# Three edits to a fp32-split streaming encoder step: queue order in the SSD chunks, block order at the start of the FFN, and the end of the last norm

## The chip, the cores and the metric

The kernel runs on one NeuronCore of one Trainium2 chip. The metric is the device time of one execution in microseconds (us). Five engines work side by side, each through its own instruction queue in order: PE (matmul; its weight loads are listed apart as PEld), DVE (VectorE), ACT (ScalarE), POOL (GpSimd) and SP (SyncE, which here only issues DMAs).

## The reference

One layer of a hybrid encoder for a prompt of 1040 rows (16 meta rows and 1024 frames) and for 8 running streams of 16 frames each, 1168 rows in all, width 1024. Stick-breaking attention and a Mamba-2 SSD branch read the same normed input, are merged with gates, and a convolutional FFN and a last norm follow. What the edits touch:

```python
# SSD branch, per chunk and head (decay exponents are <= 0)
decay_ts = exp(where(causal, a_cum[t] - a_cum[s], -inf))
y_diag   = einsum(C·B masked * decay_ts * dt[s], x)
chunk_states = einsum(to_end, B, x)            # the state's product
h        = chunk_decay * h + chunk_states      # carried from chunk to chunk
y        = y_diag + C·h_in·exp(a_cum) + d_skip * x
# FFN and last norm
u  = rms_norm(h, g_ffn);  up = causal_dwconv(u @ w_up)     # gate and val, 2816 columns each
h  = h + (silu(gate) * val) @ w_down
y  = rms_norm(h, g_final)
```

## The kernel before, in words

All large products are made of three matmuls in a rounded format: every operand is split into a high and a low part, and high·high, high·low and low·high are accumulated (`mm3`, L115, L118 and L119). A weight block of 128 columns is loaded by SP (L104), its high part made by ACT (L105) and its low part by DVE (L106). One product of such a block with a third of the rows is 24 matmuls.

The code is written for a tile framework. It plans the order of every engine's queue ahead of time: it runs the program through a simulated timeline with its own costs, and lets each engine take the instruction that is ready, earlier lines of the program first. The queues are fixed then. At run time an engine that reaches an instruction whose input has not come waits there, and all that is queued behind waits with it. Buffers of a pool are handed on in the same way: `bufs=1` or `bufs=2` says how many tiles of a name can live at a time. `issue_after(ins, prev)` adds an edge without a semaphore: the planner may not place `ins` before `prev`. Before the change it is used between instructions of one engine only.

The phases in order of time: the input norm and projections (to about 100 us), four SSD groups (to about 875 us), attention for the prompt (to about 1480 us), attention for the running streams, the merge, the output projection, the FFN (from about 2152 us) and the last norm with the output.

An SSD group convolves six blocks of 128 channels (B, C and four of x), then walks through ten chunks: the running streams' rows (chunk 9) first, then chunks 0 to 8 of the prompt, and between them `sample_state`. The large products of `z_proj` (gates) and of the next group's convolution blocks are what PE can do in between; they are called fill here. `ssd_chunk` does, in program order, with the names that the trace shows:

- L448: DMA of the exponents' rows into tile `t` (in the code `R`; four buffers, shared with `sample_state`)
- L450: C·B and the transpose of B into the PSUM tile `ms`; L454 (DVE): the masked product `cb`; L456 (ACT): the copy `bt` of B
- the transposes of x into `px` (one buffer); L462 (DVE) `xd`, L464 (POOL) `xe`
- L473 (PE): `st`, the state's product, of `xe` and `bt`; L479 (POOL) and L481 (DVE): the new state `hs`
- L483 (ACT): eight Relu instructions that clip the exponents, one per head; L484 (ACT): their Exp; L485 (DVE): the product with `cb`
- L488 (PE): `yd`; L493 and L494: DMA of `e`; L497 (PE) `yo`; L498 to L501 (DVE): the sum into x.

`out_proj(i)` makes a third of the rows of the residual, sums their squares (L1077 on ACT, L1078 on POOL), gets the inverse root (L1084, L1086, L1087) and splits the normed input of the FFN (`ph`, `pl`). `ffn_up(j)` makes block j of the gate (e = 0) and of the value (e = 1) for the three thirds. Its products go through four PSUM buffers `mm`. `ffn_last` is the last group of down projections: for each third i, eight blocks m are added to the residual (L1176), squared and summed (L1074, L1077, L1078), multiplied by the gain (L1198), transposed (`tp`, L135) and copied (L1206). Then the sum over channels is made by PE (`ss`, L1212), the inverse root by ACT and DVE (L1215 to L1217 and the four small DVE instructions of `refine`, L174 to L177), the result is scaled in three column pieces q by DVE, ACT and POOL (L1224, L1227) and written by SP (L1230, L1232).

Of the kernel before, what the change touches and what calls it, by code (L numbers as in the profile page):

```python
# [13 lines left out]
F32 = mybir.dt.float32  # L14
F32R = mybir.dt.float32r
# [62 lines left out]
class Kernel:  # L78
# [362 lines left out]
    def ssd_chunk(self, g, ch, t0, n, BT, CT, X, Hs):  # L441
# [11 lines left out]
        msk = (self.blockc if smp else self.causal)[:n, :n]  # L453
        nc.vector.tensor_tensor(out=CB[:, 0, :], in0=pc[:n, :n], in1=msk, op=ALU.mult)  # L454
        Bt = self.tile(sb, [128, 128], F32, 'bt')[:n]
        nc.scalar.copy(Bt, pc[:n, 128:256])  # L456
        px = self.tile(ps, [128, 512], F32, 'px')
        for j in range(4):
            self.T_(px[:n, 128 * j:128 * j + 128], X[j][:, ts])
# [6 lines left out]
        if smp:  # L466
            Bm = self.tile(sb, [128, 8, 128], F32, 'bm', bufs=1)
            nc.gpsimd.tensor_tensor(out=Bm, in0=Bt.unsqueeze(1).to_broadcast([128, 8, 128]),
                                    in1=self.blk.unsqueeze(2).to_broadcast([128, 8, 128]), op=ALU.mult)
        else:  # L470

            pS = self.tile(ps, [128, 512], F32, 'st')
            nc.tensor.matmul(pS, Bt, xe.rearrange("p h d -> p (h d)"), start=True, stop=True)  # L473
            Hn = self.tile(sb, [128, 512], F32, 'hs', bufs=2)
            if ch == 0:
                nc.vector.tensor_copy(Hn, pS)
            else:
                hv = lambda t: t.rearrange("p (h d) -> p h d", d=64)
                nc.gpsimd.tensor_tensor(out=hv(Hn), in0=hv(Hs), op=ALU.mult,  # L479
                                        in1=self.dec[:, ch, h0:h0 + 8].unsqueeze(2).to_broadcast([128, 8, 64]))  # L480
                nc.vector.tensor_tensor(out=Hn, in0=pS, in1=Hn, op=ALU.add)  # L481
        for h in range(8):
            nc.scalar.activation(R[:, h, :], R[:, h, :], AF.Relu, scale=-1.0, bias=tk[:, h0 + h:h0 + h + 1])  # L483
        nc.scalar.activation(R, R, AF.Exp, scale=-1.0)  # L484
        nc.vector.tensor_tensor(out=R, in0=R, in1=CB.to_broadcast([n, 8, n]), op=ALU.mult)  # L485
        yd = self.tile(ps, [128, 4, 128], F32, 'yd')
# [626 lines left out]
    def ffn_up(self, j, u2):  # L1113

        nc, a, fp = self.nc, self.a, self.fp
        cs = self.tile(fp, [128, 2, 18], F32, 'cs')
        fs = self.tile(fp, [16, 2, 128], F32, 'fs', bufs=1)
        nc.sync.dma_start(fs, a['state_ffn_conv'][0].rearrange("b i c -> (b i) c")
                          .rearrange("r (e c) -> r e c", e=2)[:, :, 128 * j:128 * j + 128])
        pf = self.tile(self.pf, [128, 512], F32, 'tp')  # L1120
        for e in range(2):
            self.T_(pf[:, 16 * e:16 * e + 16], fs[:, e])
        fi = self.tile(fp, [128, 32], F32, 'fi')
        nc.scalar.copy(fi, pf[:, :32])
        ac, act = [], []
        for e in range(2):
            blk = j + 22 * e
            w = lambda q: self.cwf[:, q * 44 + blk:q * 44 + blk + 1]
            ac.append(self.tile(fp, [128, 3, 384], F32, 'acc', bufs=3))
            W = self.weights(a['w_up'][0], 0, 8, DFF * e + 128 * j, 128)  # L1130
            for i in range(3):
                n0 = PW if i < 2 else 258
                x = self.tile(fp, [128, 402], F32, 'fx', bufs=3)
                xs = x[:, n0:].rearrange("p (b t) -> p b t", t=18) if i == 2 else None

                def evac(p, c, w_):
                    nc.scalar.copy(x[:, :n0], p[:, :n0])
                    if i == 2:
                        nc.scalar.copy(xs[:, :, 2:18], p[:, n0:w_].rearrange("p (b t) -> p b t", t=16))
                self.proj(W, u2[i], [(0, PW)], evac)  # L1140
                o = ac[e][:, i]
                parts = [(o[:, 0:n0 - 2], lambda q: x[:, q:q + n0 - 2])]
                if i == 2:
                    nc.gpsimd.tensor_copy(xs[:, :, 0:2], fi[:, 16 * e:16 * e + 16].rearrange("p (b i) -> p b i", i=2))
                    nc.gpsimd.tensor_copy(cs[:, e, 0:2], x[:, n0 - 2:n0])
                    nc.gpsimd.tensor_copy(cs[:, e, 2:18].rearrange("p (b i) -> p b i", i=2), xs[:, :, 16:18])
                    parts.append((o[:, 256:384].rearrange("p (b t) -> p b t", t=16), lambda q: xs[:, :, q:q + 16]))
                for op, src in parts:
                    nc.scalar.activation(op, src(0), AF.Identity, scale=w(0), bias=w(3))  # L1149
                    for q in (1, 2):  # L1150
                        nc.vector.scalar_tensor_tensor(out=op, in0=src(q), scalar=w(q), in1=op, op0=ALU.mult, op1=ALU.add)  # L1151
                if e == 0:
                    nc.scalar.activation(o, o, AF.Silu)
                    continue
                nc.vector.tensor_tensor(out=ac[0][:, i], in0=ac[0][:, i], in1=o, op=ALU.mult)
                act.append(tuple(self.tile(self.actp, [128, 384], F32R, n) for n in ('ah', 'al')))
                self.split(*act[i], ac[0][:, i])
        p = self.tile(self.pf, [128, 512], F32, 'tp')
        for e in range(2):
            self.T_(p[:18, 128 * e:128 * e + 128], cs[:, e, :])  # L1160
        so = self.tile(fp, [18, 256], F32, 'so', bufs=1)
        nc.scalar.copy(so, p[:18, :256])
        for e in range(2):
            cc = slice(DFF * e + 128 * j, DFF * e + 128 * j + 128)
            nc.sync.dma_start(a['ffn_conv_prompt'][0, 0][:, cc], so[0:2, 128 * e:128 * e + 128])
            nc.sync.dma_start(a['ffn_conv_sample'][0].rearrange("b i c -> (b i) c")[:, cc], so[2:18, 128 * e:128 * e + 128])
        return act
# [18 lines left out]
    def ffn_last(self, j0, act):  # L1186

        nc, a, fp = self.nc, self.a, self.fp
        for i in range(3):
            c = 384 * i  # L1190
            ss, ys, last, n = self.tile(self.pf, [128, 512], F32, 'ss', bufs=1), [], None, 0
            acc = self.tile(fp, [128, PW], F32, 'sq')[:, :384]
            for m in range(8):
                if m % 2 == 0:
                    W = self.weights(a['w_down'][0], j0, len(act), 128 * m, 256)
                h = self.down(W, act, m, i)
                self.square(acc, h, m == 0)
                nc.vector.tensor_scalar(out=h, in0=h, scalar1=self.gv[:, 24 + m:25 + m], scalar2=None, op0=ALU.mult)  # L1198
                prev, last = last, h
                for h in ([] if m == 0 else [prev]) + ([last] if m == 7 else []):  # L1200
                    pt = self.tile(self.pf, [128, 512], F32, 'tp')
                    for b in range(3):
                        self.T_(pt[:, 128 * b:128 * b + 128], h[:, 128 * b:128 * b + 128])
                    if n % 3 == 0:
                        ys.append(self.tile(fp, [128, 3, 384], F32, 'acc', bufs=3))
                    done = nc.scalar.copy(ys[-1][:, :, 128 * (n % 3):128 * (n % 3) + 128],  # L1206
                                          pt[:, :384].rearrange("p (b n) -> p b n", n=128))
                    if n == 3:
                        self.load_sqrt(fp, done)
                    n += 1  # L1210
            for b in range(3):
                nc.tensor.matmul(ss[:, b:b + 1], acc[:, 128 * b:128 * b + 128], self.ones[:, 0:1], start=True, stop=True)  # L1212
            t = self.tile(fp, [128, 2, 3], F32, 'nrm')
            s, r = t[:, 0], t[:, 1]
            nc.scalar.copy(s, ss[:, 0:3])  # L1215
            nc.scalar.activation(r, s, AF.Sqrt, bias=self.eps, scale=1.0 / D)
            nc.vector.reciprocal(r, r)  # L1217
            self.refine(fp, r, s, 1.0 / D)
            for q, y in enumerate(ys):
                k = min(384, D - 384 * q)  # L1220
                y = y[:, :, :k]
                if q == 1:
                    for b in range(3):
                        nc.scalar.activation(y[:, b], y[:, b], AF.Copy, scale=r[:, b:b + 1])  # L1224
                else:
                    eng = nc.vector if q == 0 else nc.gpsimd
                    eng.tensor_tensor(out=y, in0=y, in1=r.unsqueeze(2).to_broadcast([128, 3, k]), op=ALU.mult)  # L1227
                cs = slice(384 * q, 384 * q + k)
                nb = 3 if i < 2 else 2
                nc.sync.dma_start(a['y_prompt'][0][c:c + 128 * nb, cs].rearrange("(b p) n -> p b n", p=128), y[:, :nb])  # L1230
                if i == 2:
                    nc.sync.dma_start(a['y_sample'].rearrange("b t c -> (b t) c")[:, cs], y[:, 2])  # L1232


def body(ctx, tc, a):
# [41 lines left out]
```

## Time and profile before

| what | value |
|---|---|
| median of three runs | 3040.69 us (3036.63 to 3044.58) |
| the profiled execution | 3035.7 us, its span 3033.7 us |
| mean granted TensorE clock | 0.988 |
| busy: PE, DVE, ACT, POOL | 2926.8, 1733.1, 1262.9, 611.2 us |
| HBM traffic | 244.31 MB read, 91.15 MB written |

Times in the rows are microseconds from the start of the span. In a list of waits the columns are: the engine and what it wanted to do, what ended its wait, the sum, the count and the longest. In a timeline: start, duration, engine, line, operation, output and inputs, count, and in brackets the idle time of the engine before it and what ended it. In a table of windows: busy time of each engine with the number of its instructions, then the granted clock, the busy share of the DMA engines and GB/s.

### The profile page before, as it was taken

The numbers are of one execution on the slowest core, as the hardware profiler recorded it, in microseconds if no ns is written. First come the engines' busy times: TensorE is split into PE (matmuls) and PEld (weight loads), VectorE is DVE, ScalarE is ACT, GpSimd is POOL, SyncE is SP. The second block draws the span as 40 slices with busy tenths as digits, with TensorE's granted clock in tenths as the row PEclk, the third lists the DMA queues.
The fourth block names the chain that finished last, engine by engine and source line by source line (L and its number), as shares of the span: only waits on it lengthen the run. The fifth ranks groups of instructions, "written<-read, shape, count | busy, mean of one in ns | idle before, by whom it ended". The sixth has DMA issues, their size and how long they took to land. (4 is left out here: it accounts for less than half of the span.)

```text
span 3033.7 us, 45461 instructions
## 1 busy us (share of the span) xinstructions
PE 2926.8 (96%) x17381; PEld 2768.3 (91%) x17381; DVE 1733.1 (57%) x2625; ACT 1262.9 (42%) x2630; POOL 611.2 (20%) x967
## 2 busy tenths in 40 slices
PE   7999999999989999999799899999999999999998
PEld 5997988979879999999699899999999999999997
DVE  6467666666656777777634441346754454545447
ACT  6545435354334544554434320214534242424245
POOL 0013132131222333333323000002201010101014
PEclk9999999999999999999899999999999999999999
DMA  5436255353574554544444553536211111111113
GB/s 188 110 86 172 87 141 152 91 162 90 148 218 125 167 148 132 157 124 106 77 137 140 168 171 100 152 105 195 71 43 44 43 44 43 44 43 40 39 43 119
DMA packets 445496, 338.44 MB, mean 112 GB/s; under 512 B 43991, under 2 KB 421155, under 8 KB 445279
## 3 DMA queue, kind: packets, MB, share of 16 engines
q1 hardware_dynamic: 445279, 335.54, 38.8%
q8 instruction: 137, 2.24, 0.3%
q14 instruction: 80, 0.66, 0.1%
HBM read 244.31 MB, written 91.15 MB: 111 GB/s over the span
## 5 line engine op out<-in xcount | busy, mean ns | idle before, releaser
L115 PE MATMUL mm<-sh,wh 128*128 128x384 f32 (+3 forms) x2520 | 869.5, 346 | 14.7 <-ACT sh L942 5.2
L118 PE MATMUL mm<-sl,wh 128*128 128x384 f32 (+3 forms) x2520 | 869.8, 345 | 2.3 <-DVE sl L98 1.2
L119 PE MATMUL mm<-sh,wl 128*128 128x384 f32 (+3 forms) x2520 | 865.6, 344 | 0.0
L115 PEld LDWEIGHTS mm<-sh,wh 128*128 128x128 f32 (+1 forms) x2520 | 475.7, 189 | 29.5 <-ACT sh L942 6.4
L118 PEld LDWEIGHTS mm<-sl,wh 128*128 128x128 f32 (+1 forms) x2520 | 475.7, 189 | 15.5 <-issue 8.9
L119 PEld LDWEIGHTS mm<-sh,wl 128*128 128x128 f32 (+1 forms) x2520 | 475.5, 189 | 5.7 <-issue 3.9
L106 DVE TENSOR_TENSOR wl<-wf,wh 128x1024 fp32r<-128x1024 f32 (+2 forms) x205 | 252.6, 1233 | 318.0 <-ACT wh L105 317.8
L115 PE MATMUL mm<-ph,wh 128*128 128x386 f32 x1248 | 424.5, 340 | 2.7 <-ACT ph L97 2.0
L118 PE MATMUL mm<-pl,wh 128*128 128x386 f32 x1248 | 424.6, 341 | 0.0
L119 PE MATMUL mm<-ph,wl 128*128 128x386 f32 x1248 | 422.5, 339 | 0.2 <-DVE wl L106 0.2
L105 ACT CAST wh<-wf 128x1024 fp32r<-128x1024 f32 (+2 forms) x205 | 212.4, 1037 | 482.2 <-PE mm L118 454.5
L1151 DVE SCALAR_TENSOR_TENSOR acc<-fx,cwf,acc 128x256 f32<-128x256 f32 (+1 forms) x352 | 170.8, 516 | 154.0 <-ACT acc L1149 150.0
L115 PEld LDWEIGHTS mm<-ph,wh 128*128 128x128 f32 x1248 | 236.2, 189 | 3.9 <-ACT ph L97 2.3
L119 PEld LDWEIGHTS mm<-ph,wl 128*128 128x128 f32 x1248 | 236.2, 189 | 1.1 <-DVE wl L106 0.7
L118 PEld LDWEIGHTS mm<-pl,wh 128*128 128x128 f32 x1248 | 235.2, 188 | 1.8
L686 DVE TENSOR_TENSOR_SCAN keep<-keep 128x144 f32<-128x144 f32 (+7 forms) x128 | 179.7, 1406 | 57.9 <-POOL keep L685 57.2
L115 PE MATMUL mm<-ah,wh 128*128 128x384 f32 x528 | 179.8, 340 | 0.0
L119 PE MATMUL mm<-ah,wl 128*128 128x384 f32 x528 | 179.2, 339 | 0.0
L118 PE MATMUL mm<-al,wh 128*128 128x384 f32 x528 | 178.6, 338 | 0.0
L1078 POOL TENSOR_TENSOR sq<-sq,sq 128x386 f32<-128x386 f32 (+1 forms) x42 | 60.2, 1434 | 467.9 <-ACT sq L1077 456.4
L98 DVE TENSOR_TENSOR wTl<-wT,wTh 128x512 fp32r<-128x512 f32 (+3 forms) x176 | 103.0, 602 | 80.1 <-ACT wTh L97 79.1
L1176 DVE TENSOR_TENSOR h<-mm,h 128x384 f32<-128x384 f32 x144 | 79.8, 556 | 119.7 <-PE mm L119 119.5
(329 smaller groups left out, 4548.2 us busy)
## 6 DMA issues: line engine op xcount, KB each, us to landing
wf<-in_w_in SPq DMA_DIRECT2D x80, 512.0 KB
wf<-in_w_up SPq DMA_DIRECT2D x44, 512.0 KB
t<-s_ac SPq DMA_DIRECT2D x36, 512.0 KB
wf<-in_w_down SPq DMA_DIRECT2D x28, 512.0 KB
wf<-in_w_out SPq DMA_DIRECT2D x24, 512.0 KB
s_y<-x SPq DMA_DIRECT2D x16, 577.0 KB
yt<-s_y SPq DMA_DIRECT2D x16, 577.0 KB
KH<-s_kh SPq DMA_DIRECT2D x32, 260.0 KB
```

What stands on the lines that cost most here:

```text
L98: nc.vector.tensor_tensor(out=l, in0=x, in1=h.bitcast(F32), op=ALU.subtract)
L105: nc.scalar.copy(wh, wf)
L106: nc.vector.tensor_tensor(out=wl, in0=wf, in1=wh.bitcast(F32), op=ALU.subtract)
L115: i = nc.tensor.matmul(p, wh[:, k, :], mh[:, c:c + w], start=s, stop=False)
L118: nc.tensor.matmul(p, wh[:, k, :], ml[:, c:c + w], start=False, stop=False)
L119: nc.tensor.matmul(p, wl[:, k, :], mh[:, c:c + w], start=False, stop=e)
L686: nc.vector.tensor_tensor_scan(out=K[:, ::-1], data0=K[:, ::-1], data1=K[:, ::-1], initial=1.0, op0=ALU.mult, op1=ALU.min)
L1078: nc.gpsimd.tensor_tensor(out=acc[:, :w], in0=acc[:, :w], in1=sq, op=ALU.add)
L1151: nc.vector.scalar_tensor_tensor(out=op, in0=src(q), scalar=w(q), in1=op, op0=ALU.mult, op1=ALU.add)
L1176: self.nc.vector.tensor_tensor(out=h, in0=p, in1=h, op=ALU.add)
```

## The change

In `ssd_chunk` each of the eight Relu instructions gets an ordering edge: in the nine prompt chunks behind the state's product `st` of the same chunk, which is an instruction of PE; in the running streams' chunk behind the copy `bt`.

In `ffn_up` the two `acc` tiles and the two weight blocks (gate and value) are requested together ahead of the loop, for every j. For j = 0 the six products are made in the order gate third 0, gate third 1, value third 0, value third 1, gate third 2, value third 2; for the other j the order is as before.

In `ffn_last`, block m = 7 is no longer added to the sum of squares by POOL: PE accumulates the sum of m < 7 and the square of m = 7 into `ss` with twice the matmuls. The gain of m = 7 is applied by ACT in place of DVE. The copy of `ss` to SBUF (L1215) goes; the root and the refinement read PSUM. Piece q = 2 of the result is scaled by POOL (one of three row blocks) and DVE (two) in place of POOL alone, and the writes of piece q = 1 are issued by ACT in place of SP.

```diff
-        nc.scalar.copy(Bt, pc[:n, 128:256])
+        first = nc.scalar.copy(Bt, pc[:n, 128:256])
...
-            nc.tensor.matmul(pS, Bt, xe.rearrange("p h d -> p (h d)"), start=True, stop=True)
+            first = nc.tensor.matmul(pS, Bt, xe.rearrange("p h d -> p (h d)"), start=True, stop=True)
...
         for h in range(8):
-            nc.scalar.activation(R[:, h, :], R[:, h, :], AF.Relu, scale=-1.0, bias=tk[:, h0 + h:h0 + h + 1])
+            self.issue_after(nc.scalar.activation(R[:, h, :], R[:, h, :], AF.Relu, scale=-1.0,
+                                                  bias=tk[:, h0 + h:h0 + h + 1]), first)
...
-        ac, act = [], []
-        for e in range(2):
+        act = []
+        ac = [self.tile(fp, [128, 3, 384], F32, 'acc', bufs=3) for e in range(2)]
+        W = [self.weights(a['w_up'][0], 0, 8, DFF * e + 128 * j, 128) for e in range(2)]
+
+        for e, i in ((0, 0), (0, 1), (1, 0), (1, 1), (0, 2), (1, 2)) if j == 0 else ((e, i) for e in range(2) for i in range(3)):
...
-                self.square(acc, h, m == 0)
-                nc.vector.tensor_scalar(out=h, in0=h, scalar1=self.gv[:, 24 + m:25 + m], scalar2=None, op0=ALU.mult)
+                if m < 7:
+                    self.square(acc, h, m == 0)
+                    nc.vector.tensor_scalar(out=h, in0=h, scalar1=self.gv[:, 24 + m:25 + m], scalar2=None, op0=ALU.mult)
+                else:
+
+                    sq = self.tile(fp, [128, PW], F32, 'sq')[:, :384]
+                    nc.scalar.activation(sq, h, AF.Square)
+                    for b in range(3):
+                        for x, e in ((acc, False), (sq, True)):
+                            nc.tensor.matmul(ss[:, b:b + 1], x[:, 128 * b:128 * b + 128], self.ones[:, 0:1], start=not e, stop=e)
+                    nc.scalar.activation(h, h, AF.Copy, scale=self.gv[:, 31:32])
...
-            for b in range(3):
-                nc.tensor.matmul(ss[:, b:b + 1], acc[:, 128 * b:128 * b + 128], self.ones[:, 0:1], start=True, stop=True)
-            t = self.tile(fp, [128, 2, 3], F32, 'nrm')
-            s, r = t[:, 0], t[:, 1]
-            nc.scalar.copy(s, ss[:, 0:3])
+            s, r = ss[:, 0:3], self.tile(fp, [128, 3], F32, 'nrm')
...
-                    eng = nc.vector if q == 0 else nc.gpsimd
-                    eng.tensor_tensor(out=y, in0=y, in1=r.unsqueeze(2).to_broadcast([128, 3, k]), op=ALU.mult)
+                    for eng, b, e in ((nc.vector, 0, 3),) if q == 0 else ((nc.gpsimd, 2, 3), (nc.vector, 0, 2)):
+                        eng.tensor_tensor(out=y[:, b:e], in0=y[:, b:e], op=ALU.mult,
+                                          in1=r[:, b:e].unsqueeze(2).to_broadcast([128, e - b, k]))
...
-                nc.sync.dma_start(a['y_prompt'][0][c:c + 128 * nb, cs].rearrange("(b p) n -> p b n", p=128), y[:, :nb])
+                dma = nc.scalar if q == 1 else nc.sync
+                dma.dma_start(a['y_prompt'][0][c:c + 128 * nb, cs].rearrange("(b p) n -> p b n", p=128), y[:, :nb])
                 if i == 2:
-                    nc.sync.dma_start(a['y_sample'].rearrange("b t c -> (b t) c")[:, cs], y[:, 2])
+                    dma.dma_start(a['y_sample'].rearrange("b t c -> (b t) c")[:, cs], y[:, 2])
```

More of the change, by code (lines that the diff above doesn't have):

```diff
@@ L1124, in ffn_up @@
         nc.scalar.copy(fi, pf[:, :32])
-        ac, act = [], []
-        for e in range(2):
+        act = []
+        ac = [self.tile(fp, [128, 3, 384], F32, 'acc', bufs=3) for e in range(2)]
+        W = [self.weights(a['w_up'][0], 0, 8, DFF * e + 128 * j, 128) for e in range(2)]
+        for e, i in ((0, 0), (0, 1), (1, 0), (1, 1), (0, 2), (1, 2)) if j == 0 else ((e, i) for e in range(2) for i in range(3)):
             blk = j + 22 * e
             w = lambda q: self.cwf[:, q * 44 + blk:q * 44 + blk + 1]
[L1129 to L1142, printed above, removed]
-                if i == 2:
[L1144 to L1157, printed above, removed]
@@ new lines, in ffn_up, with evac @@
+            n0 = PW if i < 2 else 258
+            x = self.tile(fp, [128, 402], F32, 'fx', bufs=3)
+            xs = x[:, n0:].rearrange("p (b t) -> p b t", t=18) if i == 2 else None
+            def evac(p, c, w_):
+                nc.scalar.copy(x[:, :n0], p[:, :n0])
+                if i == 2:
+                    nc.scalar.copy(xs[:, :, 2:18], p[:, n0:w_].rearrange("p (b t) -> p b t", t=16))
+            self.proj(W[e], u2[i], [(0, PW)], evac)
+            o = ac[e][:, i]
+            parts = [(o[:, 0:n0 - 2], lambda q: x[:, q:q + n0 - 2])]
@@ new lines, in ffn_up @@
+            if i == 2:
+                nc.gpsimd.tensor_copy(xs[:, :, 0:2], fi[:, 16 * e:16 * e + 16].rearrange("p (b i) -> p b i", i=2))
+                nc.gpsimd.tensor_copy(cs[:, e, 0:2], x[:, n0 - 2:n0])
+                nc.gpsimd.tensor_copy(cs[:, e, 2:18].rearrange("p (b i) -> p b i", i=2), xs[:, :, 16:18])
+                parts.append((o[:, 256:384].rearrange("p (b t) -> p b t", t=16), lambda q: xs[:, :, q:q + 16]))
+            for op, src in parts:
+                nc.scalar.activation(op, src(0), AF.Identity, scale=w(0), bias=w(3))
+                for q in (1, 2):
+                    nc.vector.scalar_tensor_tensor(out=op, in0=src(q), scalar=w(q), in1=op, op0=ALU.mult, op1=ALU.add)
@@ L1158, in ffn_up @@
+            if e == 0:
+                nc.scalar.activation(o, o, AF.Silu)
+                continue
+            nc.vector.tensor_tensor(out=ac[0][:, i], in0=ac[0][:, i], in1=o, op=ALU.mult)
+            act.append(tuple(self.tile(self.actp, [128, 384], F32R, n) for n in ('ah', 'al')))
+            self.split(*act[i], ac[0][:, i])
         p = self.tile(self.pf, [128, 512], F32, 'tp')
```

## The prediction

> **What bounds the kernel now.** First the page's busy times: PE is the bound nearly everywhere, so only what lets PE wait, slows its clock or adds to its work counts.
>
> ```profile
> PE 2926.8 (96%) x17381; PEld 2768.3 (91%) x17381; DVE 1733.1 (57%) x2625; ACT 1262.9 (42%) x2630; POOL 611.2 (20%) x967
> ```
>
> Next, what PE waited for, by line. These are the rows that the change can touch.
>
> ```profile
> PE st L473 <- ACT bt L456: 11.5, 4, 5.1
> ...
> PE tp L135 <- ACT acc L1206: 3.1, 1, 3.1
> PE px L135 <- DVE xd L462: 2.9, 3, 1.0
> PE yd L488 <- DVE t L485: 2.9, 3, 1.6
> ...
> PE mm L115 <- ACT ph L97: 2.0, 1, 2.0
> ...
> PE tp L135 <- DVE h L1198: 1.4, 1, 1.4
> ...
> PE ms L536 <- ACT hT L533: 0.6, 1, 0.6
> ```
>
> The first row is the largest wait of PE in the whole list: the state's product waits for the copy of B four times, once in each SSD group. The 3.1 us ahead of `tp` (3015.7 to 3018.8) are not idle: the last block's sum reads, right after them, a product whose matmuls have no record and fill that gap:
>
> ```profile
> 3019.63 0.55 DVE L1176 TENSOR_TENSOR h<-mm,h 128x384 f32<-128x384 f32 x1
> ```
>
> Third, the timeline at the first of the four waits, engine by engine.
>
> ```profile
> 262.53 0.38 PE L450 MATMUL ms<-bc,bc 128*128 128x128 f32 x2
> ...
> 263.43 0.37 SPq L448 DMA_DIRECT2D t<-s_ac  x1
> ...
> 265.80 1.05 POOL L464 TENSOR_TENSOR xe<-xd,tok 128x512 f32<-128x512 f32 x1 [1.36 <-DVE xd L462]
> ...
> 267.87 2.45 ACT L483 ACTIVATE t<-t,tok 128x128 f32<-128x128 f32 x8 [4.44 <-DMA t<-s_ac]
> 270.22 0.24 ACT L456 COPY bt<-ms 128x128 f32<-128x128 f32 x1
> 270.37 1.06 ACT L484 ACTIVATE t<-t 128x1024 f32<-128x1024 f32 x1
> ...
> 270.61 1.10 PE L473 MATMUL st<-xe,bt 128*128 128x512 f32 x2 [1.60 <-ACT bt L456]
> ```
>
> B is transposed at 263 and `xe` is done at 266.85, yet `bt` starts at 270.22: ACT's queue holds, ahead of it, the eight Relus of the next chunk, whose exponents were asked for at 263.43 and came at 267.9. ACT stood 4.44 us at that DMA. Fourth, such places by window, with the waits of PE in group 2 ahead (640 to 655 us; group 1 has the same with 1.6 at `yd`): after the waits of groups 1, 2 and 3 the granted clock is low.
>
> ```profile
> PE st L473 <- ACT bt L456: 2.4, 1, 2.4
> ...
> PE yd L488 <- DVE t L485: 0.6, 1, 0.6
> ```
>
> ```profile
> 264.00:272.00 8.00, 5.45 (x42) 4.19 (x38) 6.47 (x13) 4.13 (x12) 3.47 (x3) 1.00 0.73 202
> 446.00:458.00 12.00, 8.25 (x61) 6.83 (x59) 8.18 (x15) 2.43 (x8) 4.28 (x3) 1.00 0.68 185
> 458.00:466.00 8.00, 6.79 (x38) 4.23 (x39) 3.51 (x5) 6.53 (x17) 2.73 (x2) 0.79 0.40 103
> ...
> 648.00:656.00 8.00, 6.90 (x39) 4.52 (x40) 3.47 (x9) 7.41 (x18) 3.00 (x2) 0.79 0.53 137
> ...
> 846.00:850.00 4.00, 4.00 (x27) 1.99 (x26) 2.92 (x8) 3.33 (x10) 1.18 (x2) 0.67 0.89 243
> ```
>
> **SSD chunks.** The edge adds no instruction and no semaphore; it moves eight Relus per chunk (and with them Exp and L485) behind the chunk's `st` in the plan, so the next chunk's Relus can no longer stand ahead of this chunk's `bt`.
>
> *The wait itself.* Without it `st` is next bounded by `xe`, which at this place was done 2.2 us before PE got there (266.85 against 269.01, the start of the 1.60 us). So the whole 11.5 us go.
>
> *The clock.* The low windows cost 8 x 0.21 + 8 x 0.21 + 4 x 0.33 = 4.7 us; in the first two PE waited 1.2 and 1.1 us anyway, which at 0.21 is 0.5, so 4.2 us of work were lost. Group 0, with 2.55 us idle in 264 to 272, kept 1.00. Without their `st` waits groups 1 and 2 keep only the `yd` and `px` waits, 1.6 + 1.0 and 0.6 + 1.0 us, no more than group 0 had. I take 4.2 us back.
>
> By the Trainium skill (TensorE: Matmul & The Clock Gate, Part 1, "What's actually happening") the clock halves only after a whole idle window of about 3.4 us. The 2.4 us waits of groups 1 and 2 were shorter and were followed by 0.79 all the same, so this trace leans against so strict a reading; by the rule only group 3's loss would come back.
>
> *What is late next.* Now Relu, Exp and L485 follow `st` in the plan and `yd` follows them: 2.45 + 1.06 + 1.22 us (the last from the row below) that earlier were done far ahead. At run time nothing holds ACT back until `st` ends, and fill stands between. Behind the Relus on ACT's queue are `hT`, the gates' tanh and the squares L580; who waits for these is PE (`hT`), and it waited 0.6 us once. Relu no longer waits at its DMA, but it now stands behind L580, which waits for DVE L576 and that for a load:
>
> ```profile
> ACT t L483 <- DMA t<-s_ac: 90.5, 28, 9.1
> ...
> ACT zf L580 <- DVE x L576: 38.7, 21, 4.8
> ...
> DVE x L576 <- DMA zf<-s_z: 29.0, 13, 4.5
> ...
> 262.36 1.22 DVE L485 TENSOR_TENSOR t<-t,cb 128x1024 f32<-128x1024 f32 x1
> ```
>
> No row shows the new `yd` wait. Its ends: the 5.8 us of the `yd` and `px` rows vanish too, or each group gets two waits like the largest, 4 x 2 x 1.6 = 12.8 us. I take one of 1.0 us in each group, +4.0, nearest to the `px` row, which stands at the same place. The DMA of the exponents moves later on SP too, since its buffer is free only after a later `yd`; the chunk whose exponents came at 267.9 had its `st` 18 us later, so 5 us less is covered:
>
> ```profile
> 285.93 1.02 PE L473 MATMUL st<-xe,bt 128*128 128x512 f32 x2
> ```
>
> A group's end comes up to 4.7 us later; the next group's B and C blocks are fill there. In group 3 it is the second head pair's projection.
>
> **FFN's first block.** PE runs out after gate thirds 0 and 1, since third 2's input needs the root, the reciprocal and the split.
>
> ```profile
> 2150.00:2200.00 50.00, 47.99 (x271) 46.73 (x270) 30.71 (x54) 26.81 (x53) 7.95 (x12) 1.00 0.15 44
> 2200.00:2250.00 50.00, 50.00 (x286) 49.16 (x285) 29.57 (x56) 18.79 (x40) 2.60 (x9) 1.00 0.12 34
> ...
> 2163.86 0.62 PE L115 MATMUL mm<-ph,wh 128*128 128x386 f32 x2 [2.01 <-ACT ph L97]
> ...
> 2169.30 0.48 ACT L1137 COPY fx<-mm 128x386 f32<-128x386 f32 x1
> ```
>
> Two value products, 48 matmuls at 50/286 = 0.175 us, are 8.4 us of work from 2161.9 to 2170.3. That covers the 2.0 us: -2.0 (ends 0, and -2.6 from 15 missing matmuls in the window). PSUM is just enough: four products lie in four buffers, and the first is copied out by 2169.8, 0.5 us before the fifth starts. Asking for both weight blocks at once puts one load on SP, one cast on ACT and one subtraction on DVE ahead of the gate's copies; ACT and DVE are at most 61% busy there and PE has three finished products in reserve, so nothing. With that cover gone it would be the cast's 1 us per block.
>
> **The last norm.** The steps of the last third, and one `ss` in the middle of the work:
>
> ```profile
> 2981.51 0.50 PE L1212 MATMUL ss<-ones,sq 128*128 128x1 f32 x4
> ...
> 3020.27 0.52 ACT L1077 ACTIVATE sq<-h 128x384 f32<-128x384 f32 x1 [0.37 <-DVE h L1176]
> ...
> 3020.87 0.99 POOL L1078 TENSOR_TENSOR sq<-sq,sq 128x384 f32<-128x384 f32 x1 [1.38 <-ACT sq L1077]
> ...
> 3022.89 1.28 PE L1212 MATMUL ss<-ones,sq 128*128 128x1 f32 x6
> ...
> 3024.21 0.16 ACT L1215 COPY nrm<-ss 128x3 f32<-128x3 f32 x1 [0.59 <-PE ss L1212]
> ...
> 3025.78 2.59 POOL L1227 TENSOR_TENSOR acc<-acc,nrm 128x768 f32<-128x768 f32 x1 [3.92 <-issue]
> ...
> 3026.82 0.89 SPq L1230 DMA_DIRECT2D out_y_prompt<-acc  x2
> ...
> GB/s 0 0 0 0 11 0 0 0 21 0 163 351 379 357 359 346 75 0 0 0 0 0 0 0 0 0 0 0 0 0 0 34 359 369 377 357 341 194 0 0
> ```
>
> The six squared passes start at 3020.9 instead of 3022.89 (POOL's sum goes, DVE's gain with its 1.4 us wait no longer stands ahead of them) and L1215 with its gap, 0.19, goes: the root comes 2.2 us earlier. The passes of the sum of m < 7 fit under the square if the planner takes them first; left between, they cost 0.9. Behind the root, shorter scaling (POOL 256 of 768 columns) and the issues from ACT only bring the writes together: they already ran at 341 to 377 GB/s without a hole, so the end moves by the 2.2 us and no more. Against it stands that thirds 0 and 1 get six more passes each where PE is full, 12 x 0.125 = 1.5 us. Together -0.7 (ends -2.2 and +1.5). ACT's DMA issues, 0.4 us each, and gain, 0.5, lie in thirds 0 and 1 beside PE's work.
>
> **The sum.** -11.5 - 4.2 + 4.0 - 2.0 - 0.7 = -14.4 us. The profiled execution took 3035.7 us (span 3033.7 and 2.0 around it) and would take 3021.3; it lies 5.0 us below the median of the three runs, so against 3040.7 I forecast 3026.3 us.
>
> **The rivals.**
> 1. Slower: `yd` becomes the wait that `st` was. ACT's three steps (4.7 us) now lie in each chunk's path, and where ACT stands at L580 PE stands at `yd`. For it: 38.7 us of ACT's waits behind L576. Against it: PE's waits for ACT's `hT` are 0.6 us in all, and the 90.5 us of waits at the exponents' DMA go. The change saves 18.4 us elsewhere; over 36 prompt chunks it turns slower above 0.51 us per chunk. With 1.6 us at every second chunk: 28.8 - 18.4 = +10.4, 3051 us.
> 2. No effect in the chunks: the edge crosses engines, so the planner may heed it and still put `bt` behind another waiting instruction such as L580, or not heed it. For it: every earlier edge joins instructions of one engine. Against it: in the shown wait it was the Relus alone. Then only -2.0 and -0.7: 3038 us.
> 3. The clock does not come back in groups 1 and 2, because short idle times do not set it: -11.5 - 1.3 + 4.0 - 2.0 - 0.7, 3029 us. For it: group 0 idled 2.55 us at 1.00. Against it: 0.79 right after both waits. The page named above would decide this way.
>
> **How the numbers follow.** Less than 0.3% (9.1 us) cannot be told from no change here, so faster is below 3031.6 and slower above 3049.8. Forecast 0.58, own range 3016 to 3034 (0.50 faster, 0.07 same, 0.01 slower); rival 1 0.16 (0.06 same, 0.10 slower); rival 2 0.18 (0.04, 0.13, 0.01); rival 3 0.08 (0.06 faster, 0.02 same). That is 0.60, 0.28 and 0.12. The best ends give -11.5 - 4.7 - 5.8 - 2.6 - 2.2 = -26.8, 3014; the worst of the forecast -11.5 + 12.8 + 1.5 = +2.8 with no clock back, 3043. The range is 3012 to 3046; above it lies most of rival 1, some 0.12.
>
> **What would show it.** Right: no wait of `st` for `bt`; in ACT's queue each chunk's L456 ahead of the next chunk's L483; clock 1.00 at those four places; no wait at `ph`; the root some 2 us after the last square. Wrong: rows `yd` <- L485 above 5 us in sum (rival 1), `st` <- `bt` still near 11 (rival 2), low clock in spite of gone waits (rival 3), or new waits in attention, which the planner orders anew too.

## The result, and the profile after

Against runs of the kernel before on the same chip (median 3038.66 us) the changed kernel takes 2996.00 us, 2993.68 to 2998.96: ratio 0.9857, 95% interval 0.9841 to 0.9872, 42.7 us less. The forecast was 3026.3 us in a range from 3012 to 3046, so the direction was right and the size far too small; the time lies 16 us below the range. The profiled execution took 2993.68 us with a span of 2991.6 us, against 3033.7 us before.

Where it came from, by the start of marked instructions in the two traces (us from the span's start):

| | before | after | gained so far |
|---|---|---|---|
| first copy of a convolution product | 104.45 | 105.21 | -0.8 |
| first product of attention (`z`) | 904.40 | 875.16 | 29.2 |
| last product of prompt attention | 1478.77 | 1444.53 | 34.2 |
| last sum of the output projection | 2152.34 | 2116.98 | 35.4 |
| first sum of the down projection | 2234.41 | 2196.73 | 37.7 |
| last sum of the down projection | 3019.63 | 2980.06 | 39.6 |
| end of the span | 3033.65 | 2991.61 | 42.0 |

Of the 42.0 us of the two spans 30.0 came between the first copy of a convolution product and attention, that is from the SSD groups, where the prediction had 11.7. First PE's busy time on the page of the changed kernel; PE has 11.6 us less of it than before (2926.8), although the last norm gives it a few more instructions:

```profile
PE 2915.2 (97%) x17399; PEld 2766.0 (92%) x17399; DVE 1711.6 (57%) x2625; ACT 1263.0 (42%) x2630; POOL 610.3 (20%) x964
```

Then all that PE waited for from 100 to 876 us after (line, releaser, us in total, times, longest):

```profile
PE yo L499 <- DVE hs L481: 2.5, 2, 1.8
PE st L473 <- ACT zf L582: 1.6, 1, 1.6
PE ms L135 <- ACT st L659: 1.2, 2, 1.0
PE mm L115 <- ACT xp L368: 0.9, 3, 0.5
```

The waits of `st` for `bt` (11.5 us), of `px` for `xd` (2.9) and of `yd` for L485 (2.9) are gone, and `yd` waits nowhere. The list of before, over 100 to 905 us, held further rows, which the prediction did not quote. The largest of them, and the second largest of the whole stretch, is this:

```profile
PE mm L115 <- ACT xp L368: 4.4, 2, 3.5
```

Those 3.5 us stand at 115 us, in the convolution that opens the first group. ACT's timeline of before at that place, and PE's:

```profile
113.68 3.84 ACT L483 ACTIVATE t<-t,tok 128x128 f32<-128x128 f32 x15 [3.26 <-DMA t<-s_ac]
117.42 1.03 ACT L105 CAST wh<-wf 128x1024 fp32r<-128x1024 f32 x1
118.36 0.37 ACT L366 COPY xp<-mm 128x272 f32<-128x272 f32 x1
118.63 0.26 ACT L368 COPY xp<-mm 128x128 f32<-128x128 f32 x1
...
118.94 0.69 PE L115 MATMUL mm<-sh,wh 128*128 128x384 f32 x1 [3.53 <-ACT xp L368]
119.43 0.52 PE L118 MATMUL mm<-sl,wh 128*128 128x384 f32 x1
```

It is the mechanism of the prediction at another victim: ACT stands 3.26 us at the DMA of exponents that nobody needs for another 80 us, and behind the 15 Relus stand the copies that free PE's PSUM buffers. The matmuls after it take 0.52 us instead of 0.34: the granted clock has fallen to half (0.50 from 118.2 to 125.0 us). Stage windows (length, busy us of PE, PEld, DVE, ACT, POOL, granted clock, DMA share, GB/s), first of before, then of after:

```profile
104.00:190.00 86.00, 82.47 (x463) 81.23 (x461) 42.25 (x52) 46.23 (x103) 8.79 (x23) 0.96 0.32 85
381.00:475.00 94.00, 89.04 (x613) 73.92 (x612) 64.41 (x111) 39.31 (x96) 33.47 (x27) 0.98 0.55 149
572.00:664.00 92.00, 87.93 (x607) 73.20 (x606) 62.76 (x111) 38.96 (x95) 34.23 (x27) 0.98 0.56 152
741.00:874.00 133.00, 125.80 (x841) 107.23 (x840) 87.90 (x148) 52.09 (x118) 40.03 (x32) 0.99 0.48 133
```

```profile
105.00:190.00 85.00, 85.00 (x493) 83.77 (x491) 45.02 (x56) 36.46 (x70) 8.21 (x24) 1.00 0.35 94
373.00:457.00 84.00, 84.00 (x597) 71.18 (x596) 55.74 (x100) 42.41 (x109) 32.33 (x24) 1.00 0.54 148
558.00:641.00 83.00, 83.00 (x591) 70.43 (x591) 54.94 (x99) 42.02 (x108) 32.32 (x24) 1.00 0.52 149
721.00:850.00 129.00, 127.20 (x871) 110.36 (x870) 88.79 (x152) 63.57 (x156) 43.42 (x34) 1.00 0.54 149
```

PE's idle time between the first convolution copy and attention fell from 24.9 to 6.4 us (gaps of the PE rows), and the lost clock, 86 x 0.04 + 94 x 0.02 + 92 x 0.02 + 133 x 0.01 = 8.5 us, is back (a little less counts, since PE was idle in 1.0 us of that time). That is some 27 of the 30.0 us that this stretch became shorter.

ACT tells the same from its side. In before its largest wait in this stretch was the one at the exponents' DMA. In after the group of these Relus has no idle time ahead of it at all:

```profile
ACT t L483 <- DMA t<-s_ac: 93.7, 29, 9.1
```

```profile
L484 ACT ACTIVATE t<-t,tok 128x128 f32<-128x128 f32 (+1 forms) x320 | 94.7, 381 | 0.0
L490 PE MATMUL yd<-t,xd 128*64 128x128 f32 (+1 forms) x640 | 41.9, 272 | 0.0
```

Attention gave 5.0 us more, most of it at its opening, which no edit touches. In before its second `z` and the transposes of the weights waited, and the clock fell; in after more large products stand between them, and the waits are shorter:

```profile
910.26 0.45 PE L719 MATMUL z<-KH,QS 128*128 128x400 f32 x1 [1.79 <-ACT beta L682]
912.09 0.41 PE L135 MATMUL wT<-ident,beta 128*128 128x128 f32 x2 [0.95 <-DVE beta L688]
...
912.00:916.00 4.00, 3.41 (x14) 3.18 (x15) 2.55 (x5) 0.48 (x1) 1.24 (x3) 0.68 0.51 137
```

```profile
879.84 0.45 PE L721 MATMUL z<-KH,QS 128*128 128x400 f32 x1 [0.45 <-ACT beta L684]
883.11 0.44 PE L135 MATMUL wT<-ident,beta 128*128 128x128 f32 x2 [0.21 <-DVE beta L690]
...
883.00:887.00 4.00, 3.89 (x24) 3.89 (x25) 2.25 (x5) 1.23 (x3) 0.93 (x2) 1.00 1.02 319
```

From 3 us ahead of the first `z` to 12 us behind it PE has 34 matmuls of large products in before and 54 in after. The planner orders the whole program anew after an edit, and here the new order happens to leave more filler.

The FFN's first block has no gap any more, 50.00 us busy of 50 where it was 47.99. The end of the kernel is told below, with the runs on the last norm.

### The profile page after: what moved, and what is told of

It reads as the page before. It is cut to its first block, busy times and chain, and to the rows that moved or that the text cites. A ratio compares the mean times of both kernels' runs of the same rounds, so it can differ in the third digit from the quotient of the medians.

```text
span 2991.6 us, 45527 instructions
## 1 busy us (share of the span) xinstructions
PE 2915.2 (97%) x17399; PEld 2766.0 (92%) x17399; DVE 1711.6 (57%) x2625; ACT 1263.0 (42%) x2630; POOL 610.3 (20%) x964
## 5 line engine op out<-in xcount | busy, mean ns | idle before, releaser
L1153 DVE SCALAR_TENSOR_TENSOR acc<-fx,cwf,acc 128x384 f32<-128x384 f32 (+1 forms) x352 | 170.8, 515 | 155.5 <-ACT acc L1151 151.7
L1178 DVE TENSOR_TENSOR h<-mm,h 128x384 f32<-128x384 f32 x144 | 79.7, 555 | 120.0 <-PE mm L119 119.5
```

What stands on the lines that cost most here:

```text
L1178: self.nc.vector.tensor_tensor(out=h, in0=p, in1=h, op=ALU.add)
```

## The experiments

Each kernel is named with what it differs in. The times and ratios are against the kernel before in the same set of runs. The theory (A) is: ACT's queue stands at the exponents' DMA, and everything behind it on ACT, not `bt` alone, reaches PE late; the edge moves the Relus to where the DMA has long landed.

**The edge alone** (`first` and the `issue_after` around the Relu, as in the change; FFN and norm as before).

> The kernel before with the ordering edges of the SSD chunks alone. Theory A (ACT's queue): the 94 us that ACT stood at the exponents' DMA held up everything queued behind, the copy of B, but also the copies of the convolution's products and the gates' steps; without them PE's idle time up to attention falls from 24.7 to about 6 us and the low clock goes, so -34 to -38 us against the kernel before (about 3003), with no row of the Relu at its DMA. Theory B (what the prediction said): the edges give only the four waits for the copy of B and the clock after them, -12 to -16 us (about 3024), and the rest of the 42 us comes from the other two edits.

3001.64 us against 3035.21, ratio 0.9890 [0.9875, 0.9905]: 33.6 us less, as theory A expected. The first `z` comes 30.0 us earlier, attention takes 4.4 us less, and the rest 1.5 us less.

**FFN's first block alone.**

> The kernel before with the FFN edit alone (first block's order, both weight blocks and both accumulators asked for together). Theory A: -2.0 to -2.6 us, the wait of PE for the third input (2.0 us) gone, nothing else moved: about 3036. Theory B: the earlier weight blocks also change the later blocks, -5 us or more.

3032.94 us, ratio 0.9991 [0.9982, 1.0000]: 2.3 us less. The interval touches no change, but the profile puts the gain where it was expected: from the last sum of the output projection to the first of the down projection 79.7 us, 82.1 before.

**The last norm alone.**

> The kernel before with the last norm's edit alone. Theory A: the root comes 2.4 us earlier after the last block's sum, and the last blocks, which DVE and POOL and not PE pace, gain another 1 to 2 us, the extra sums of PE cost nothing there: -3.5 to -4.5 us, about 3034.5. Theory B (the prediction): -2.2 on the last chain and +1.5 for the extra passes, -0.7 us, about 3038.

3031.14 us, ratio 0.9984 [0.9975, 0.9992]: 4.1 us less. The three parts give 33.6 + 2.3 + 4.1 = 40.0 of the 42.7 us, so they nearly add up. One reason for the rest is in the traces: in the kernels with the edge alone and with the norm alone the wait of 2.0 us in the FFN's first block is followed by half clock, and that stretch takes 83.6 us where it took 82.1 in before; the FFN's edit is worth 1.5 us more there. From the last sum (3017.49) to the end of the span are 11.6 us, 14.0 before, and from the last sum of the down projection's second third to that of its last third it takes 19.32 us, 21.24 before: two gains, of which the prediction had only the first.

**The edge behind the copy of B only**, so that the Relus may still stand ahead of the state's product. Against the edge alone:

```diff
-            first = nc.tensor.matmul(pS, Bt, ...)     # the edge is to the copy of B alone
+            nc.tensor.matmul(pS, Bt, ...)
```

> The kernel before with the Relus of every chunk ordered behind the copy of B of the same chunk (both on ACT) and not behind the state's product on PE. Theory A: the exponents have landed long before the copy of B, so ACT waits at no DMA either and nearly all of the gain of the edges stays: -28 to -38 us, about 3006. Rival C: it is the place behind the state's product that counts, since it also keeps ACT free while the product's inputs are made: less than half of it, about 3024 or slower.

3009.04 us, ratio 0.9912 [0.9898, 0.9926], 26.2 us less. The first `z` comes 29.0 us earlier, nearly as with the full edge, and PE has no gap over 0.25 us until 867 us. So the place behind `st` is not what counts in the groups; it is enough that the Relus leave the head of the queue. What is missing goes mostly at attention's beginning, where this order has two waits and a halved clock:

```profile
PE ms L135 <- ACT rows L643: 3.6, 1, 3.6
PE ms L135 <- ACT rows L633: 2.6, 1, 2.6
...
871.00:875.00 4.00, 1.27 (x5) 0.87 (x6) 1.22 (x1) 1.85 (x4) 0.00 (x0) 0.50 1.04 347
```

**The edge in one kind of chunk only.** Chunk 9, the running streams' 8 x 16 = 128 rows (not 16, as the expectation has it), or the prompt's nine chunks:

```diff
-            nc.scalar.activation(R[:, h, :], ..., AF.Relu, ...)
+            relu = nc.scalar.activation(R[:, h, :], ..., AF.Relu, ...)
+            if smp:              # chunk 9; in the other kernel: if not smp
+                self.issue_after(relu, first)
```

> The kernel before with the order edge only in chunk 9 of each group (the 16 running tokens): there the Relus stand behind the copy of B, in the prompt's nine chunks they stand where they were. Theory A (an ACT queue that stops at the exponents' DMA): chunk 9 opens a group and its load is the first one after the convolution, so this edge alone removes the 3.5 us wait of the convolution at 115.4 us of the profile and the clock that it costs: the first product of group 0's chunks comes 5 to 6 us earlier (195.6 to 190), and the time falls by 5 to 9 us. Rival E (the prompt's chunks alone matter): under 3 us.

> The kernel before with the order edge only in the nine prompt chunks of each group (Relus behind the state's product); chunk 9 is as before. Theory A: the rest of the edge's gain of 33.6 us, so 25 to 29 us faster, and with the chunk 9 edge's gain the sum is 33.6 within 4 us; the wait at 115.4 us stays. Rival E: 31 us or more, the whole gain.

Chunk 9 alone: 3037.12 us, ratio 1.0008 [0.9998, 1.0017], nothing gained. The prompt's chunks alone: 3000.51 us, 0.9892 [0.9877, 0.9907], the whole gain. By the time theory A's split was wrong and rival E right. At the place itself theory A was nearly right. With the edge in chunk 9, ACT and PE there:

```profile
114.13 1.70 ACT L483 ACTIVATE t<-t,tok 16x16 f32<-16x16 f32 x8 [3.41 <-DMA t<-s_ac]
117.25 0.44 PE L115 MATMUL mm<-sh,wh 128*128 128x384 f32 x1 [0.98 <-ACT xp L368]
```

At 114 us now the eight Relus of a prompt chunk (the one of 16 rows) stand at the DMA, for 3.41 us instead of 3.26, but they alone stand ahead of the copies. PE's wait is 0.98 us where it was 3.53, the clock stays at 1.00, and the first product of the chunks comes at 191.57 us, 4.0 us earlier (5 to 6 were expected). The gain is lost again behind it: from that product to the first `z` it takes 712.3 us, 708.8 before, and PE's idle time up to attention is 25.9 us in all, with new rows at `st` and `ms`. ACT's waits at the exponents are 96.0 us in this kernel, 93.7 before. With the edge in the prompt's chunks they are 6.0 us; the convolution's wait stays there, 2.34 us, as theory A said, but with no clock lost behind it. Taking away one early wait leaves a queue of others behind it; they must all be held.

**No transfer to wait for**, without and with the three edits:

```diff
-        nc.sync.dma_start(R, self.s_ac[h0:h0 + 8, ts].partition_broadcast(n))
...
-            ... nc.scalar.activation(R[:, h, :], R[:, h, :], AF.Relu, ...)
+            ... nc.scalar.activation(R[:, h, :], self.causal[:n, :n], AF.Relu, ...)
```

> The kernel before, with the loading of the exponents left out: the Relus read a constant mask in SBUF in place of the loaded rows, so that they never wait for a transfer (40 transfers, 36 of 512 KB, are gone; the decay factors are not the reference's). The order of the instructions is that of before. Theory A: ACT's 93.7 us of waits for these transfers are gone, and with them the whole gain of the edge: 30 to 38 us faster than before. Rival D (the Relus' own ACT time ahead of the copies of B, of px and of the convolution is what costs, 3.1 us in each chunk, whatever the transfer does): under 14 us faster.

> The changed kernel with the loading of the exponents left out in the same way. Theory A: its Relus do not wait for the transfers anyway, so it stands within 5 us of the changed kernel (38 to 48 us faster than before), and only the 6 to 10 us of the FFN's first block and the last norm ahead of the kernel before without loading. Rival D: it stands 25 us or more ahead of the kernel before without loading. Rival F (the transfers themselves cost, as bandwidth): over 10 us faster than the changed kernel.

Before without the loading: 3012.43 us against 3034.83, ratio 0.9936 [0.9921, 0.9951], 22.4 us less. The changed kernel without it: 3001.05 us, 0.9893 [0.9877, 0.9910], 33.8 us less, where the changed kernel with its loading gave 42.7; theory A had 38 to 48. It stands 11.4 us ahead of the other one, where theory A had 6 to 10 and rival D 25 or more. By the time alone the kernel before without loading lies between theory A (30 to 38) and rival D (under 14); the traces decide. One statement of the expectation does not hold: the order is not quite that of before, since the planner reacts to the missing transfer too. But what rival D needs is there: the median chunk's first Relu starts 29.5 us ahead of its copy of B (24.4 in before, 1.5 us behind it in after), so the Relus' own time on ACT still lies ahead of the copies. The Relus do not run freely either: they now stand for their buffers `t`, for which SP stood in before, ahead of the DMA (52.8 us for `yd`, 20.0 for `out_ssm_sample`). ACT's list over 100 to 905 us:

```profile
ACT t L482 <- PE yd L487: 24.1, 13, 3.7
ACT t L482 <- DMA out_ssm_sample<-t: 16.8, 9, 3.5
```

PE's waits up to attention nearly vanish all the same, to 3.9 us of idle time, and its clock is 1.00 from the first convolution copy to there:

```profile
PE mm L115 <- ACT xp L366: 1.4, 1, 1.4
PE ms L135 <- ACT st L656: 1.0, 1, 1.0
PE ms L449 <- DVE t L551: 0.5, 1, 0.5
```

Attention begins at 878.65 us without the edits and at 877.87 with them. Where there is no transfer to wait for, the change moves this point by 0.8 us; where there is, by 29.2. That is the test of theory A, and rival D falls. Rival F falls as well: 36 transfers of 512 KB less bring the changed kernel no gain. Two things are left over. Without the loading, 3 us of the gain at attention's begin are missing, in the kernel before spread over PE's busy time, in the changed kernel as some 9 us of waits from 864 to 877 us; and attention's opening has gaps like those of before (1.90 and 0.88 us in the kernel before). They do not lie at the exponents and may come from the order as newly planned; no run isolates them.

**The loading twice**, as a larger dose of the wait (the `dma_start` of L448 stands twice):

> The kernel before with each load of the exponents issued twice in a row into the same tile, so that the rows are there a transfer later (20 MB more are moved). Theory A (ACT stops at the transfer and the copies behind it stop PE): ACT's 93.7 us of waits for these transfers grow past 150 us, and the time by 15 us or more over before. Rival G (what the edges gain comes from the order of the instructions as it is planned anew, not from the transfer): the same small change as for the changed kernel, the two within 8 us of each other.

> The changed kernel with each load of the exponents issued twice. Theory A: its Relus stand behind the state's product, which comes long after the transfer, so there is cover for a second one: under 8 us slower than the changed kernel, with little or no wait of ACT for the transfers. Rival G: as much slower as the kernel before becomes.

3093.37 us, ratio 1.0189 [1.0173, 1.0205], and 3046.30 us, 1.0033 [1.0022, 1.0045]: 57 us over before, 50 over the changed kernel. By these times rival G would be right, and theory A's "under 8 us" is wrong. The dose was not clean, though. The second load writes the same tile, so SP itself stands until the first has landed, and what is queued on SP behind it stands too. SP's and ACT's waits of the changed kernel with two loads, over 100 to 930 us:

```profile
SPq L449 <- DMA t<-s_ac: 115.7, 33, 6.9
...
ACT zf L583 <- DVE x L579: 110.0, 24, 8.8
DVE x L579 <- DMA zf<-s_z: 89.5, 20, 7.8
```

ACT's wait at the exponents is not in its list, as theory A says (175.6 us in before with two loads, as it says too); but the gates' loads are late now (52.8 us with one load), and ACT stands there. The pair shows that the same head-of-queue trouble can be made on SP. It does not weigh A against G. The pair without loading does, and so do all fourteen traces together. In the five kernels where ACT stands 83 us or more at the exponents, PE's idle time up to attention is 24.0 to 25.9 us (64.8 with two loads); in the eight where it stands 6.0 us or not at all, with one load or none, it is 3.9 to 10.1 us. These eight have their edges in different places, or no edge and no load, so this is not one lucky order. Only the changed kernel with two loads stands apart: no such wait of ACT, and 44.4 us idle, beside the waits of SP shown here.

**The last third's gain on ACT** (four blocks), and **one pass of sums in the first two thirds**:

```diff
+                    if i == 2 and m >= 3:
+                        nc.scalar.activation(h, h, AF.Copy, scale=self.gv[:, 24 + m:25 + m])
```

```diff
-                if m < 7:
+                if m < 7 or i < 2:       # thirds 0 and 1: three products with the ones, as before
```

> The changed kernel with the gain multiplication of blocks 3 to 6 of the last third on ACT (0.6 us) in place of DVE, where it takes 1.25 us beside POOL; the order ahead of that is the same. If DVE's sums and gains pace the last blocks, block 7 of the last third comes earlier by 0.5 to 1.5 us (19.35 us lie between the last h of the second third and that of the last) and the time falls by as much. If PE's products pace them (19.3 us is their own time), no change within 0.4 us of the profile.

> The changed kernel with the old single pass of sums (three products with the ones, one accumulator over all eight blocks) in the first two thirds; only the last third takes the short chain. The prediction charged the six extra passes with 1.5 us. If it was right, the last h of the second third comes 1 to 1.5 us earlier against the first down product; if the passes fill time that PE has anyway, under 0.4 us, and the time stays.

With the gain on ACT: 2994.85 us against 3036.25, ratio 0.9861 [0.9841, 0.9880]. The last third takes 18.67 us instead of 19.35, 0.7 less, within what was expected, and PE ends at 2982.20 us, just ahead of the last sum's start at 2982.24; this is not told from the changed kernel's time by these runs. With one pass of sums: 3000.21 us, 0.9884 [0.9869, 0.9899], and the last two thirds take 21.71 + 21.35 us instead of 21.15 + 19.35. That is 2.6 us more, and the expectation's two cases, 1 to 1.5 us earlier or no change, were both wrong. The run does not isolate the passes, since with them block 7's gain goes back to DVE and its square to POOL in these thirds: the first sum of the last third then starts 2.68 us after the last one of the second third, with the short chain 1.60 us. So the six extra passes cost nothing that shows, and what gains is the short chain on DVE and POOL. DVE and POOL show how the last third runs with the short chain everywhere (changed kernel, then the one with one pass):

```profile
2972.72 0.54 DVE L1178 TENSOR_TENSOR h<-mm,h 128x384 f32<-128x384 f32 x1
2973.19 1.27 DVE L1201 TENSOR_SCALAR h<-h,gv 128x384 f32<-128x384 f32 x1
2974.38 0.55 DVE L1178 TENSOR_TENSOR h<-mm,h 128x384 f32<-128x384 f32 x1
...
2973.22 1.02 POOL L1080 TENSOR_TENSOR sq<-sq,sq 128x384 f32<-128x384 f32 x1 [0.64 <-ACT sq L1079]
```

```profile
2983.99 0.55 DVE L1178 TENSOR_TENSOR h<-mm,h 128x384 f32<-128x384 f32 x1
2985.18 1.26 DVE L1201 TENSOR_SCALAR h<-h,gv 128x384 f32<-128x384 f32 x1 [0.65 <-ACT sq L1079]
2986.36 0.55 DVE L1178 TENSOR_TENSOR h<-mm,h 128x384 f32<-128x384 f32 x1
...
2985.57 0.93 PE L135 MATMUL tp<-ident,h 128*128 128x128 f32 x6 [3.50 <-ACT acc L1217]
```

In the slow rhythm (before, and one pass) a block goes sum, square on ACT, gain, next sum: 2.37 us here, and DVE is idle 0.65 us in it. In the fast one the gain follows its sum at once and overlaps the square of a neighbouring block, 1.66 us here; the last block takes 2.4 us in both. PE's gap of 3.5 us near the end is back with one pass: PE had its products done and the blocks behind them were late.

## Why the prediction was wrong in size

*The step that failed first: "the four waits of `st`" as the whole of the queue's cost.* The reading of the queue was right (edge in, `bt` free, no semaphore needed), and so were the 11.5 us: all gone. But the 93.7 us that ACT stood at the exponents (90.5 in the prediction's window, which began at 190 us, behind the convolution's wait) were priced by one victim. The same Relus held the copies of the convolution (3.5 us) and, with it, 3.4 us of clock (86 x 0.04), and the waits at `px` and `yd`, 5.8 us, were an end of a range and not the value taken. Measured for the edges alone: 33.6 us, against a forecast of 11.5 + 4.2 - 4.0 = 11.7. Up to attention, the changed kernel's trace has 18.5 us less of idle time and 8.5 us of clock back. Of the 28.3 us between forecast and measurement (42.7 against 14.4) 21.9 are the edges, 3.4 the last norm, 0.3 the FFN, and 2.7 what the parts give only together.

*The new waits of `yd`, +4.0.* They did not come: L490 has no idle time. After the edge the Exp of the median chunk starts 7.3 us ahead of its `yd`; before it was 24.2 us ahead. The slack shrank as said, and what was left was enough. ACT does stand longer for the product of DVE L578 (51.4 us at L582, 38.7 before), as the prediction feared, but that wait reaches PE once, for 1.6 us.

*The clock, -4.2.* It came back at all three places, and at a fourth that the prediction had not looked at. Rival 3 (it doesn't come back) is out; so are rival 1 (`yd` waits) and rival 2 (no effect).

*FFN, -2.0.* Right: 2.3 us in the run alone, and 2.3 us in the trace.

*The last norm, -0.7.* Measured 4.1 us. The shorter chain was right: from the last sum to the end 11.55 us instead of 14.02, 2.5 where 2.2 was forecast, with the writes as before at 354 to 366 GB/s at their height. Two things were wrong. The 3.1 us ahead of `tp` were taken for products without records. They were idle: the 528 rows of each of the three matmul lines are complete, PE's last product ended at 3015.72 us, and its sum on DVE, at 3019.63, was late by itself. With the short chain the gap is gone.

```profile
3015.39 0.34 PE L119 MATMUL mm<-ah,wl 128*128 128x384 f32 x1
3018.83 1.60 PE L135 MATMUL tp<-ident,h 128*128 128x128 f32 x7 [3.11 <-ACT acc L1206]
```

And the 1.5 us for twelve extra passes were charged to a PE that in this stretch waits for DVE: the second third takes 21.15 us without them (before) and with them (after).

*Attention, not forecast.* The warning was there ("which the planner orders anew too") and no price. Prompt attention took 574.4 us in before, 569.4 in after, 570.0 with the edge alone, 570.1 with that of the prompt's chunks, but 573.0 with the edge behind `bt` and 574.1 in the changed kernel without the loading. It follows the order that the planner arrives at (53 to 55 products at the opening in the first three with the edge, 35 and 27 in the last two). Over all fourteen traces it falls from 573 to 576 us with 27 to 35 such products to 568 to 569 with 58 to 60. Whether the edge behind `st` brings that order about or chance does stays open.

One caution on such numbers: the kernel with the gain on ACT has the same order as the changed kernel up to the end of the FFN, and its first `z` came 3.4 us later; 2.6 us of that are busy time of PE, which had half clock in two places where the changed kernel had none. So a difference of 3 us between two single profiles over the SSD stretch says nothing of the edit.

## What to carry to other kernels

An engine's wait at a DMA is priced by everything that stands behind it in that queue, not by the largest row of the bound engine's waits: list all waits of PE in the stretch, and follow each back to the same blocked queue. When early-ready work is let in ahead of urgent work, hold all of that kind back: held in one chunk of ten it gained 4 us at that place and nothing in the end. And a gap that the trace shows idle is to be counted against the complete number of records before it is explained away.

## What the runs showed of the hardware

*The clock after the same gap.* With the same order of instructions and the same wait of 1.64 us at `st` (837.89 us in the changed kernel, 840.18 in the one with the gain on ACT), the granted clock stayed at 1.00 after one and was halved after the other. In these traces the granted clock changes only on a grid of 3.41 us, which lies differently against the program in each run. By the slots of this grid, changed kernel first:

```profile
833.74:837.15 3.41, 2.48 (x14) 1.90 (x13) 2.76 (x5) 1.84 (x3) 1.46 (x2) 1.00 0.32 116
837.15:840.57 3.42, 2.67 (x20) 1.97 (x22) 2.48 (x3) 3.34 (x10) 3.42 (x3) 1.00 0.30 86
840.57:843.98 3.41, 3.41 (x28) 2.59 (x24) 3.41 (x6) 2.78 (x5) 0.39 (x1) 1.00 0.47 127
```

```profile
837.33:840.74 3.41, 1.71 (x9) 0.93 (x8) 3.41 (x5) 3.00 (x7) 2.76 (x3) 1.00 0.16 58
840.74:844.15 3.41, 3.41 (x14) 2.46 (x14) 2.04 (x4) 3.41 (x10) 2.50 (x2) 0.50 0.21 58
844.15:847.57 3.42, 3.42 (x29) 2.74 (x28) 3.42 (x5) 1.50 (x3) 0.00 (x0) 1.00 0.66 166
```

The wait lies across two slots in the first kernel (PE idle 0.93 and 0.75 us in them) and within one in the second (1.70), and the next slot there runs at 0.50. From 100 to 1440 us of all fourteen traces no slot at full clock with less than 1.65 us of idle PE is followed by half clock, and none with more than 1.84 us is followed by full clock; between the two both occur. Behind 1440 us slots with 1.0 us idle were followed by half clock too, so this is no more than what these stretches show. So a short gap costs up to 1.7 us of clock (half of 3.41) or none, by where it falls on the grid, and a gap removed saves this risk too. The Trainium skill (TensorE: Matmul & The Clock Gate, Part 1, "What's actually happening") says that the activity window runs freely and doesn't start with the kernel; this fits the grid. That a whole window of 3.4 us must be idle does not fit the 1.70 us.

*DVE beside POOL.* The gain on DVE took 0.42 us where POOL did nothing (the first block of a third, which has no sum of squares) and 1.25 to 1.28 us where POOL's sum of squares, 1.0 us, started within 0.05 us of it. In the changed kernel's last group of down projections 17 gains overlap such a sum, and 16 of them end 0.22 us behind it, wherever it started (the last: gain at 2978.87 for 1.27 us, sum at 2978.91 for 1.00 us). Once, in before, the sum started 0.10 us behind the gain; there the gain took 0.42 us and the sum 1.21. The Trainium skill (SBUF — State Buffer, "SBUF: two separate sides") says that DVE and GpSimd share a port pair that, for DVE instructions of some kinds, one of them holds for a whole instruction while the other waits. These rows agree that one waited for the other; no run here changes that alone.
